# Two more features of each MLP's first group as half-size products, and the second mixer's block masks built from iotas in the second group

## The chip, the core and the metric

One NeuronCore of one Trainium2 chip runs the whole program. Its engines run side by side, each with a queue of its own: TensorE (PE: matrix products), VectorE (DVE), ScalarE (ACT), GpSimd (POOL), and SyncE (SP), which orders most DMAs. The metric is the device time of one execution in microseconds. The kernel before took 1311.64 us (median of three runs, 1311.3 to 1313.36).

## What is computed

Two residual layers of an encoder on 512 tokens of width 1024 in float32. Layer 0 mixes tokens with a bidirectional gated DeltaNet, layer 1 with gated linear attention (GLA). Behind each mixer comes a squared-ReLU MLP with 4096 features:

```python
def _sq_relu_mlp(h, w1, w2):
    a = jax.nn.relu(jnp.matmul(h, w1))
    return jnp.matmul(a * a, w2)

for i in range(DEPTH):                      # DEPTH = 2
    m = _mixer_gdn(...) if i % 2 == 0 else _mixer_gla(...)
    x = _layernorm(ALPHA * x + m, ln1_g[i], ln1_b[i])
    x = _layernorm(ALPHA * x + _sq_relu_mlp(x, mlp_w1[i], mlp_w2[i]), ln2_g[i], ln2_b[i])
```

GLA has a lower-triangular score matrix per chunk that the kernel builds by levels (blocks of 1, 2, 4 up to 64 positions); at each level a 0/1 mask of a 128x128 tile says which scores the level sets.

## The kernel before

**Split products.** Every float32 operand is split into a high half (a cast to fp32r, by ScalarE, L102) and a low half (what is left, by VectorE, L107). A product is then three matmuls: high by high, low by high, high by low (`mm3`, L128 to L130).

**The MLP** (function `mlp`) works in four groups of 1024 features; a group has 8 "features" (tiles of 128), f = 0 to 7 in the code. The up projection turns x (transposed, halves `xth` and `xtl`) into h; the down projection sums w2 times h into the residual `xt`.

- In groups 1 to 3 the up projection takes features in pairs (class `Pair`). Two features, the two halves of the 1024 inputs and the two halves of the 512 tokens make a 2x2 by 2x2 block product, and Strassen's scheme (in Winograd's form) does it in seven half-size products instead of eight. Each is 12 matmuls of 128x256. They are issued in the order 1, 2, 6, 5, 7, 3, 4; the text calls them P1 to P7. Their results go to two PSUM banks of tag `pj`, named `fx` and `fyz`. The products need sums of the blocks of x (`x_blocks`: four sums of high and low, L433, four combinations, L439 to L442, four splits into `xh` and `xl`), made once per MLP, and sums of the blocks of the weights, made per pair: `prepare` splits the first weight tile (P1, P2), forms four sums (L464) and splits one more half tile (P5, L470 and L471), then adds the last sum; `late(0, (6, 4))`, called by `finish`, splits the sum for P6 and P4; `late(1, (7, 3))` the one for P7 and P3.
- In group 0 the features 0 to 3 are computed as ordinary products in two halves of the tokens (`proj_halves`), and 4 to 7 one by one (`feature`): 8 tiles of the inputs by 3 matmuls of 128x512. Bank tag `pj`, results read by ScalarE (Relu L383, Square L384). While these run, VectorE and ScalarE make the x blocks and prepare the first pair.
- The down projection (`second`, `last`) uses the same scheme on the 2x2 blocks of h and w2, in seven products of four chunks of six matmuls of 128x512 (banks `pX`, `pY`, `pZ`). Blocks of w2 lie in tiles `w2r`, loaded by SyncE; their sums are formed by DMAs that GpSimd orders and that add in flight (L415). `split(1)` makes the halves (`w2h`, `w2l`) for the first product, `pair` those of h (`ah`, `al`).
- Chunks of group g's down projection are interleaved with products of group g+1 on TensorE.

**The order.** The code is recorded, and a scheduler then orders each engine's queue; `issue_after` and `high_priority` bend that. `in_order` pins the recorded order on one engine. Weight tiles come into a ring of three buffers (`wst`), halves go to a ring of three (`wh`, `wl`), and SyncE waits in its queue for a buffer to be free.

**The masks** (function `sel_masks`, called by `GlaConst` through `extra` of the first MLP): for each block size GpSimd fills a 128x128 tile with ones, cuts it twice by an affine select, subtracts the one before and casts to bytes. The call stands behind group 0; GpSimd starts it when the first MLP does.

Of the kernel before, what the change touches and what calls it, by code (L numbers as in the profile page):

```python
# [351 lines left out]
def mlp(c, w1, w2, g, b, out=None, extra=None, room=0):  # L352
# [14 lines left out]
    with c.banks(pj=2, X=2, Y=2, Z=2), tc.tile_pool(name="mlp", bufs=2) as pool:  # L367
# [333 lines left out]
        todo = [(gi, p) for gi in range(1, G) for p in range(GF // 2)]  # L701
# [23 lines left out]
        for f in range(4, GF):  # L725
            feature(0, f, h)
            if f >= 5:
                next(xb)
            if f == 4:
                load(0, 0, 0)  # L730
            if f == 5:
                load(0, 0, 1)
            if f == 6:
                load(0, 1, 1)
                with tc.issue_after(c.last_hi.ins), tc.issue_after(c.last_lo.ins):
                    split(1)
                a = pair(quarters(h)[0])
        begin(0)
        prepare(0)
        finish(0)  # L740
        if extra:
            extra(lambda: pool.tile([P, P], F32, name="tmp", tag="tmp", bufs=2))
        def stream(gi, nh):

            for p in range(GF // 2):
                i = (gi - 1) * (GF // 2) + p
                for n, _ in enumerate(ready[i].products(nh)):
                    if n == 0:
                        begin(i + 1)
                    elif n == 1:  # L750
                        ready[i].late(1, (7, 3))
                    elif n == 3:
                        prepare(i + 1)
                    elif n == 5:
                        finish(i + 1)
                    if p == 3 and n == 2 and gi + 1 == G:
                        load(gi, 1, 0, c.wst)
                    if p == 3 and n == 2:
                        split(1, None if gi + 1 < G else True)
                        stream.a = pair(quarters(nh)[0])  # L760
                    yield

        for gi in range(G - 1):
# [4 lines left out]
            with c.in_order(mybir.EngineType.PE):  # L768
                for i, _ in enumerate(second(gi, h, a)):
                    upto = n if i + 1 == m else min(i + 2, 7 * (i // 7) + 7) if i % 7 in (0, 2, 4, 6) else k  # L770
                    while k < upto:
                        next(more, None)
                        k += 1
                for _ in more:
                    pass
            h, a = nh, stream.a
        with c.in_order(mybir.EngineType.PE):
            norm, normed = last(G - 1, h, a)
# [6 lines left out]
def sel_masks(c, pool, tmp):  # L785

    nc = c.nc
    out = {}
    prev = None
    for w in (1, 2, 4, 8, 16, 32, 64, 128):  # L790
        f = tmp().rearrange("p (a b) -> p a b", b=w)
        nc.gpsimd.memset(f, 1.0)
        if w < P:
            nc.gpsimd.affine_select(out=f, in_=f, compare_op=ALU.is_ge, fill=0.0, base=0,
                                    pattern=[[-w, P // w], [0, w]], channel_multiplier=1)
            nc.gpsimd.affine_select(out=f, in_=f, compare_op=ALU.is_ge, fill=0.0, base=w - 1,
                                    pattern=[[w, P // w], [0, w]], channel_multiplier=-1)
        fl = f.rearrange("p a b -> p (a b)")
        if w != 2:
            m = pool.tile([P, P], mybir.dt.uint8, name=f"mu{w}", tag=f"mu{w}", bufs=1)  # L800
            if w == 1:
                nc.gpsimd.tensor_copy(m, fl)
            else:
                nc.gpsimd.tensor_tensor(prev, fl, prev, ALU.subtract)
                nc.gpsimd.tensor_copy(m, prev)
            out[w // 2] = m
        prev = fl
# [1106 lines left out]
```

## Time and profile before

| what | us |
|---|---|
| median of three runs | 1311.64 |
| the profiled execution | 1311.28 |
| its span on the core | 1309.6 |
| first MLP: features 4 to 7 of group 0 | 431.92 to 453.97 |
| second MLP: features 4 to 7 of group 0 | 1005.01 to 1027.09 |
| GpSimd building masks | 415.0 to 449.2 |
| first use of a mask by VectorE (L1042) | 760.3 |

The profile names a group of instructions by line, engine, operation and tiles (`out<-in`), with count, busy time and mean duration; `[x <-ENGINE tile line]` behind an instruction is the idle time of its engine just ahead of it and what ended that. A timeline gives the start and the duration of each instruction. A matmul's duration overlaps the next one's, so distances between starts tell its price. The windows give busy time of each engine between two moments.

### The profile page before, as it was taken

Reading aid. Unit: us, or ns where it says so; the run is one execution under the profiler, and the core shown is the slowest. Engines: PE = TensorE matmul, PEld = TensorE weight load, DVE = VectorE, ACT = ScalarE, POOL = GpSimd, SP = SyncE. Lnnn points to the kernel's source line nnn. Section 1 sums busy time; section 2 is a strip of 40 time slices with the busy share of each in tenths; the row PEclk is TensorE's granted clock in tenths of the full one; section 3 lists DMA queues with packets and bytes.
Section 4 is the critical chain, followed back from the end, with each engine's and each line's share of the span. In section 5 each row is a group of like instructions: output and inputs, shape, how many; then the busy total and the mean of one; then the engine's idle time right before and its main releaser. Section 6 shows DMA issues by size and latency. Waiting matters only on the chain.

```text
span 1309.6 us, 22228 instructions
## 1 busy us (share of the span) xinstructions
PE 1289.4 (98%) x8586; PEld 1106.3 (84%) x8586; DVE 1106.3 (84%) x1795; ACT 804.8 (61%) x1604; POOL 134.6 (10%) x190
## 2 busy tenths in 40 slices
PE   8999999999999999999999999999999999999996
PEld 6778888788878899999998888888888899999985
DVE  7888888988868998999989697877888789989987
ACT  5767676677543656666657754564456566666656
POOL 5000000000003710101102100000000001101021
PEclk9999999999999999999999999999999999999998
DMA  5333313233332664576647521211316376556565
GB/s 191 99 106 96 98 55 108 81 114 96 114 110 84 175 172 169 119 203 161 177 145 154 140 97 56 74 62 52 103 59 218 87 210 165 142 176 139 171 143 144
DMA packets 47805, 165.92 MB, mean 127 GB/s; under 512 B 5923, under 2 KB 6611, under 8 KB 47699
## 3 DMA queue, kind: packets, MB, share of 16 engines
q1 hardware_dynamic: 33603, 114.52, 25.8%
q0 software_dynamic: 13984, 49.95, 18.7%
q8 instruction: 67, 1.10, 0.3%
q14 instruction: 39, 0.32, 0.1%
q10 hardware_dynamic: 112, 0.03, 0.0%
HBM read 125.00 MB, written 2.65 MB: 97 GB/s over the span
## 4 chain that ended last, share of the span: by engine, by line
PE 91%; ACT 3%; DVE 3%; issue 1%; DMA 1%; SPq 0%; DVEq 0%; ACTq 0%
PE pjv L128 3%; PE pjv L129 3%; PE pjv L130 3%; PE pX L130 3%; PE pX L129 3%; PE fx L130 3%; PE fx L128 3%; PE fx L129 3%; PE pX L128 3%; PE m L1776 3%; PE fyz L128 3%; PE fyz L130 3%; PE fyz L129 3%; PE pY L129 2%; PE pY L130 2%; PE pY L128 2%
## 5 line engine op out<-in xcount | busy, mean ns | idle before, releaser
L102 ACT CAST wh<-wst 128x1024 fp32r<-128x1024 f32 x151 | 158.5, 1050 | 104.8 <-PE fyz L129 28.2
L107 DVE TENSOR_TENSOR wl<-wst,wh 128x1024 fp32r<-128x1024 f32 x149 | 183.2, 1232 | 40.3 <-ACT wh L102 40.2
L107 DVE TENSOR_TENSOR w2l<-w2r,w2h 128x1024 fp32r<-128x1024 f32 x92 | 111.5, 1222 | 21.6 <-ACT w2h L102 21.6
L102 ACT CAST w2h<-w2r 128x1024 fp32r<-128x1024 f32 x94 | 98.4, 1048 | 42.5 <-DMA w2r<-w2r 22.8
L415 POOL DMA_DIRECT2D w2r<-w2r x56 | 47.9, 887 | 492.9 <-DVE w2l L107 388.0
L464 DVE TENSOR_TENSOR wst<-wst 128x512 f32<-128x512 f32 x120 | 80.0, 687 | 0.8
L102 ACT CAST ah<-h 128x1024 fp32r<-128x1024 f32 x56 | 58.8, 1050 | 30.6 <-PE pY L129 12.0
L107 DVE TENSOR_TENSOR al<-h,ah 128x1024 fp32r<-128x1024 f32 x56 | 68.4, 1221 | 6.6 <-ACT ah L102 6.6
L130 PE MATMUL pX<-w2h,al 128*128 128x512 f32 x168 | 66.3, 394 | 0.0
L129 PE MATMUL pX<-w2l,ah 128*128 128x512 f32 x168 | 65.9, 392 | 0.0
L128 PE MATMUL pX<-w2h,ah 128*128 128x512 f32 x168 | 65.5, 390 | 0.0
L128 PE MATMUL pjv<-wh,xth 128*128 128x512 f32 x128 | 54.7, 428 | 0.0
L130 PE MATMUL fyz<-xh,wl 128*128 128x256 f32 x192 | 53.5, 278 | 0.0
L130 PE MATMUL fx<-xth,wl 128*128 128x256 f32 x192 | 53.4, 278 | 0.0
L128 PE MATMUL fyz<-xh,wh 128*128 128x256 f32 x192 | 53.4, 278 | 0.0
L128 PE MATMUL fx<-xth,wh 128*128 128x256 f32 x192 | 53.2, 277 | 0.0
L130 PE MATMUL fx<-xh,wl 128*128 128x256 f32 x192 | 53.2, 277 | 0.0
L129 PE MATMUL fx<-xtl,wh 128*128 128x256 f32 x192 | 53.2, 277 | 0.0
L129 PE MATMUL fyz<-xl,wh 128*128 128x256 f32 x192 | 53.1, 277 | 0.0
L129 PE MATMUL fx<-xl,wh 128*128 128x256 f32 x192 | 53.1, 277 | 0.0
L128 PE MATMUL fx<-xh,wh 128*128 128x256 f32 x192 | 53.1, 277 | 0.0
L129 PE MATMUL pj<-xtl,wh 128*128 128x256 f32 (+1 forms) x160 | 52.0, 326 | 0.2 <-DVE xtl L194 0.2
(542 smaller groups left out, 4312.7 us busy)
## 6 DMA issues: line engine op xcount, KB each, us to landing
wst<-in_w SPq DMA_DIRECT2D x68, 512.0 KB, 4.6
w2r<-in_w SPq DMA_DIRECT2D x60, 512.0 KB, 4.6
w2r<-w2r POOLq DMA_DIRECT2D x56, 512.0 KB, 5.7
wst<-in_a_in SPq DMA_DIRECT2D x31, 512.0 KB, 4.1
wst<-in_b_vr SPq DMA_DIRECT2D x16, 512.0 KB, 3.3
wst<-in_a_out SPq DMA_DIRECT2D x8, 512.0 KB, 4.6
wst<-in_b_in SPq DMA_DIRECT2D x8, 512.0 KB, 3.4
wst<-in_b_out SPq DMA_DIRECT2D x8, 512.0 KB, 3.2
```

Of the source, the lines that this page charges most:

```text
L102: h = nc.scalar.copy(hi, src)
L107: self.halves = h, nc.vector.tensor_tensor(lo, src, hi.bitcast(F32), ALU.subtract)
L128: mm(ps, ah, bh, start=start, stop=False, **kw)
L129: mm(ps, ah, bl, start=False, stop=False, **kw)
L130: self.last_mm = mm(ps, al, bh, start=False, stop=stop, **kw)
L415: nc.gpsimd.dma_start(blocks[a + (q,)], blocks[b + (q,)], accum_op=ALU.add)
L464: plus = lambda a, b: V.tensor_tensor(a, a, b, ALU.add)
L1776: T.matmul(ps[:, d, :], *ops(d), start=True, stop=True)
```

## The change

Features 6 and 7 of group 0 become a pair: it stands first in the list of pairs (`todo`), and its seven products run right behind feature 5, with no chunks between. The steps that prepare the following pair (`begin`, `late`, `prepare`, `finish`) are called from the pair's products as in the later groups (`step`). Two calls of `x_blocks` move ahead by a feature, and the loads and the split of the first w2 blocks move behind `finish(0)`. One `in_order` now spans TensorE's whole stretch from these products to the end of the down projection. The masks are built differently: GpSimd writes the block number of each column with an iota, VectorE shifts the row numbers into block numbers of the rows, and one VectorE comparison per level gives the mask (equal for blocks of 1, unequal for the larger ones). This is called in the second group (gi == 0, behind its chunks, issued after the first split there). Only the first MLP builds masks; both MLPs get the new pair.

```diff
-        todo = [(gi, p) for gi in range(1, G) for p in range(GF // 2)]
+        todo = [(0, GF // 2 - 1)] + [(gi, p) for gi in range(1, G) for p in range(GF // 2)]
...
+        def step(i, n):
+            if n == 0:
+                begin(i + 1)
+            elif n == 1:
+                ready[i].late(1, (7, 3))
+            elif n == 3:
+                prepare(i + 1)
+            elif n == 5:
+                finish(i + 1)
+
-        for f in range(4, GF):
+        for f in (4, 5):
             feature(0, f, h)
-            if f >= 5:
-                next(xb)
-            if f == 4:
-                load(0, 0, 0)
-            if f == 5:
-                load(0, 0, 1)
-            if f == 6:
-                load(0, 1, 1)
-                with tc.issue_after(c.last_hi.ins), tc.issue_after(c.last_lo.ins):
-                    split(1)
-                a = pair(quarters(h)[0])
+            next(xb)
+            load(0, 0, f - 4)
         begin(0)
+        next(xb)
         prepare(0)
         finish(0)
-        if extra:
-            extra(lambda: pool.tile([P, P], F32, name="tmp", tag="tmp", bufs=2))
+        load(0, 1, 1)
+        with tc.issue_after(c.last_hi.ins), tc.issue_after(c.last_lo.ins):
+            split(1)
+        a = pair(quarters(h)[0])
+        whole = contextlib.ExitStack()
+        whole.enter_context(c.in_order(mybir.EngineType.PE))
+        for n, _ in enumerate(ready[0].products(h)):
+            step(0, n)
...
+            if extra and gi == 0:
+                with tc.issue_after(c.halves[1].ins):
+                    extra(lambda: pool.tile([P, P], F32, name="tmp", tag="tmp", bufs=2))
...
+    G.iota(pi, pattern=[[0, n]], base=0, channel_multiplier=1)
+    for k in range(1, n):
+        V.tensor_scalar(pi[:, k:k + 1], pi[:, k:k + 1], k, None, ALU.arith_shift_right)
+    V.tensor_copy(pf, pi)
...
+    for k in range(n):
+        w = 1 << k
+        f = tmp()
+        G.iota(f.rearrange("p (a b) -> p a b", b=w), pattern=[[1, P // w], [0, w]], base=0, channel_multiplier=0,
+               allow_small_or_imprecise_dtypes=True)
+        m = out[w if k else 0] = pool.tile([P, P], mybir.dt.uint8, name=f"mu{w}", tag=f"mu{w}", bufs=1)
+        V.tensor_scalar(m, f, pf[:, k:k + 1], None, ALU.not_equal if k else ALU.is_equal)
```

**VectorE, first MLP, from the last combination of x blocks.** In the kernel before (`xl` low halves of the x blocks, `wl` of up-projection weights, `al` of h, `w2l` of w2; L464 the sums of the pair's weights):

```order
L442 SCALAR_TENSOR_TENSOR w2r<-w2r 128x1024
L107 TENSOR_TENSOR al<-h,ah 128x1024
L107 TENSOR_TENSOR wl<-wst,wh 128x1024
L107 TENSOR_TENSOR xl_6041<-w2r,xh_6040 128x1024
L107 TENSOR_TENSOR xl_6045<-w2r,xh_6044 128x1024
L107 TENSOR_TENSOR xl_6049<-w2r,xh_6048 128x1024
L107 TENSOR_TENSOR wl<-wst,wh 128x1024
L464 TENSOR_TENSOR wst<-wst 128x512 x4
L107 TENSOR_TENSOR w2l<-w2r,w2h 128x1024
L471 TENSOR_TENSOR wl<-wst,wh 128x512
L464 TENSOR_TENSOR wst<-wst 128x512
L107 TENSOR_TENSOR wl<-wst,wh 128x1024
```

In the changed kernel, from the same instruction to the low half for P6 (the last row):

```order
L442 SCALAR_TENSOR_TENSOR w2r<-w2r 128x1024
L107 TENSOR_TENSOR wl<-wst,wh 128x1024
L107 TENSOR_TENSOR xl_5961<-w2r,xh_5960 128x1024
L107 TENSOR_TENSOR xl_5969<-w2r,xh_5968 128x1024
L464 TENSOR_TENSOR wst<-wst 128x512
L107 TENSOR_TENSOR w2l<-w2r,w2h 128x1024
L464 TENSOR_TENSOR wst<-wst 128x512 x2
L471 TENSOR_TENSOR wl<-wst,wh 128x512
L464 TENSOR_TENSOR wst<-wst 128x512 x2
L107 TENSOR_TENSOR w2l<-w2r,w2h 128x1024
L107 TENSOR_TENSOR al<-h,ah 128x1024
L107 TENSOR_TENSOR wl<-wst,wh 128x1024
```

The low halves of features 6 and 7 are gone from this queue, and the splits for the down projection (`w2l`, `al`) now stand between the pair's sums and P6's low half. From the first L433 to that row, the changed queue holds 18 instructions of 1024 elements and 6 of 512. In the second MLP P6's low half has 20 of 1024 and 6 of 512 ahead of it from the first L433 on, two of them splits that stood elsewhere.

**ScalarE, first MLP, from the Relu of the last feature before the pair's half tile.** In the kernel before (`wh` L470 the half tile of the pair, Relu L383 and Square L384 of features 6 and 7 around it):

```order
L383 ACTIVATE h<-pj 128x512
L384 ACTIVATE h<-h 128x512
L102 CAST w2h<-w2r 128x1024
L470 CAST wh<-wst 128x512
L383 ACTIVATE h<-pj 128x512
L384 ACTIVATE h<-h 128x512
L102 CAST wh<-wst 128x1024
L383 ACTIVATE h<-pj 128x512
```

In the changed kernel (the first Relu is feature 4's, the second feature 5's; the `w2h` is the first half of the block of the down projection's second product, the `wh` behind the second Relu the high half for P6, L499 and L506 copy P1 and P6):

```order
L383 ACTIVATE h<-pj 128x512
L384 ACTIVATE h<-h 128x512
L470 CAST wh<-wst 128x512
L102 CAST w2h<-w2r 128x1024
L383 ACTIVATE h<-pj 128x512
L102 CAST wh<-wst 128x1024
L384 ACTIVATE h<-h 128x512
L499 COPY h<-fx 128x256
L102 CAST wh<-wst 128x1024
L522 ACTIVATE h<-h 128x256
L506 COPY h<-fx 128x256
```

The cast of `w2h` now stands ahead of the Relu that frees P2's bank and of P6's high half; its block is ordered by SyncE when the third x block has been split. In the second MLP the same cast stands ahead of L470 and of both Relus, and the high half for P6 ahead of feature 5's Relu.

**VectorE, start of the second group of the first MLP.** In the kernel before (`wl` of the next pair, L577 and L579 combinations of the blocks of h, L503 adds P2):

```order
L107 TENSOR_TENSOR w2l<-w2r,w2h 128x1024
L107 TENSOR_TENSOR wl<-wst,wh 128x1024
L577 TENSOR_TENSOR h<-h 128x4x256
L107 TENSOR_TENSOR al<-h,ah 128x1024
L503 TENSOR_TENSOR h<-h,fyz 128x256
L579 SCALAR_TENSOR_TENSOR h<-h 128x4x256
L107 TENSOR_TENSOR wl<-wst,wh 128x1024
L107 TENSOR_TENSOR w2l<-w2r,w2h 128x1024
```

In the changed kernel (`pi` the row numbers, `pf` the same as float, `tmp` the iotas, `mu` the masks; three more comparisons follow):

```order
L797 TENSOR_SCALAR pi<-pi 128x1 x6
L577 TENSOR_TENSOR h<-h 128x4x256
L798 CAST pf<-pi 128x7
L107 TENSOR_TENSOR al<-h,ah 128x1024
L503 TENSOR_TENSOR h<-h,fyz 128x256
L806 TENSOR_SCALAR mu_6931<-tmp,pf 128x128
L806 TENSOR_SCALAR mu_6935<-tmp,pf 128x128
L107 TENSOR_TENSOR wl<-wst,wh 128x1024
L806 TENSOR_SCALAR mu_6939<-tmp,pf 128x128
L806 TENSOR_SCALAR mu_6943<-tmp,pf 128x128
L107 TENSOR_TENSOR w2l<-w2r,w2h 128x1024
```

The mask work stands between the splits, and L579 has moved behind all seven comparisons. The first two iotas are made when the MLP starts; the other five wait for a comparison to free a tile. On TensorE the order differs in one place per MLP: 84 matmuls of 128x256 (`fx`, `fyz`) where 48 of 128x512 (`pj`) stood, between feature 5 and the first `pX`.

More of the change, by code (lines that the diff above doesn't have):

```diff
@@ L767, in mlp @@
             m = 24 if gi + 2 == G else 28
[L768 to L775, printed above, removed]
-            h, a = nh, stream.a
-        with c.in_order(mybir.EngineType.PE):
-            norm, normed = last(G - 1, h, a)
+            for i, _ in enumerate(second(gi, h, a)):
+                upto = n if i + 1 == m else min(i + 2, 7 * (i // 7) + 7) if i % 7 in (0, 2, 4, 6) else k
+                while k < upto:
+                    next(more, None)
+                    k += 1
+            for _ in more:
+                pass
+            h, a = nh, stream.a
+            if extra and gi == 0:
+                with tc.issue_after(c.halves[1].ins):
+                    extra(lambda: pool.tile([P, P], F32, name="tmp", tag="tmp", bufs=2))
+        norm, normed = last(G - 1, h, a)
+        whole.close()
         with contextlib.nullcontext() if out is not None else tc.issue_after(normed[1].ins):
```

35 lines of the change are left out of this document (6 added, 29 removed).

## The prediction

> **What bounds the kernel now.** I read the page's first part, then the table of windows over the stretch that changes, then TensorE's timeline there.
>
> ```profile
> PE 1289.4 (98%) x8586; PEld 1106.3 (84%) x8586; DVE 1106.3 (84%) x1795; ACT 804.8 (61%) x1604; POOL 134.6 (10%) x190
> PE 91%; ACT 3%; DVE 3%; issue 1%; DMA 1%; SPq 0%; DVEq 0%; ACTq 0%
> ...
> core 0: us, PE busy (x) PEld busy (x) DVE busy (x) ACT busy (x) POOL busy (x), PEclk, DMA share, GB/s
> 432.00:454.00 22.00, 22.00 (x98) 18.03 (x97) 20.90 (x20) 13.11 (x18) 17.79 (x21) 1.00 0.64 195
> 532.00:572.00 40.00, 40.00 (x263) 36.29 (x262) 36.95 (x46) 25.51 (x37) 4.25 (x5) 1.00 0.66 160
> 572.00:612.00 40.00, 40.00 (x266) 36.42 (x265) 36.13 (x45) 26.17 (x38) 2.56 (x3) 1.00 0.62 171
> 1005.00:1028.00 23.00, 23.00 (x102) 18.82 (x101) 13.13 (x14) 11.84 (x16) 1.70 (x2) 1.00 0.76 230
> ```
>
> TensorE has 91% of the chain that ended last, and in the MLPs it is busy in every microsecond of these windows at full clock. So a matmul removed there is worth its own time, and any new wait is worth its own length. The windows also show the difference on which this case turns. In the first MLP (432 to 454 us) VectorE is busy 20.90 of 22 us; in the second (1005 to 1028) 13.13 of 23.
>
> **What goes: matmul time.** TensorE's timeline gives the starts: features 6 and 7 of the first group, the chunk of the down projection behind them, then P1, P2 of the next pair and the chunk behind (columns: start, duration, engine, line, operation).
>
> ```profile
> 442.94 0.40 PE L128 MATMUL pj<-xth,wh 128*128 128x512 f32 x1
> 453.97 0.39 PE L128 MATMUL pX<-w2h,ah 128*128 128x512 f32 x1
> ...
> 455.36 0.28 PE L128 MATMUL fx<-xth,wh 128*128 128x256 f32 x1
> 456.72 0.28 PE L128 MATMUL fyz<-xth,wh 128*128 128x256 f32 x1
> 458.09 0.39 PE L128 MATMUL pX<-w2h,ah 128*128 128x512 f32 x1
> ...
> 1016.08 0.39 PE L128 MATMUL pj<-xth,wh 128*128 128x512 f32 x1
> 1027.09 0.39 PE L128 MATMUL pX<-w2h,ah 128*128 128x512 f32 x1
> ```
>
> The two features take 453.97 - 442.94 = 11.03 us (second MLP 11.01), which is 48 matmuls of 512 columns at 0.230 us. A product of 12 matmuls of 256 columns takes (458.09 - 455.36) / 2 = 1.365 us, 0.114 us each, so seven take 9.55 us. The gain is 1.48 us per MLP, **2.95 us** in both, if TensorE never waits.
>
> The Trainium skill (TensorE: Matmul & The Clock Gate, section Back-to-back issue gap) speaks against such halving. It gives about 81 ns per matmul at 128 columns and about 131 at 512 in a sustained stream; interpolated, an estimate of mine, 256 columns would take 98, three quarters of a full one, and the seven products would lose 84 x 0.098 - 48 x 0.131 = 1.9 us per MLP. The trace here does not agree: its matmuls are in proportion to their columns (0.114 against 0.230), both widths are in its rows, and so this gets no chance of its own.
>
> **What comes: VectorE's chain to P6 in the first MLP.** Features 6 and 7 were also the 11 us in which VectorE finished the sums of x and the weights of the first pair. P6, third product, needs its low half of the weights (the last row of the new VectorE order shown ahead) 2 x 1.365 us and two matmuls after P1. P1 starts where feature 6 did, at 442.94, so this low half is due at 442.94 + 2.73 + 0.23 = 445.9. From the first sum of x (L433) the new order has 18 instructions of 1024 elements and 6 of 512 ahead of it. Their pace:
>
> ```profile
> 421.94 3.92 DVE L433 TENSOR_TENSOR w2r<-xth,xtl 128x1024 f32<-128x1024 f32 x3
> ...
> 1000.27 1.22 DVE L107 TENSOR_TENSOR xl<-w2r,xh 128x1024 fp32r<-128x1024 f32 x1
> 1001.41 1.22 DVE L107 TENSOR_TENSOR wl<-wst,wh 128x1024 fp32r<-128x1024 f32 x1
> ...
> 468.55 1.28 DVE L464 TENSOR_TENSOR wst<-wst 128x512 f32<-128x512 f32 x2
> ...
> 455.08 1.23 DVE L107 TENSOR_TENSOR wl<-wst,wh 128x1024 fp32r<-128x1024 f32 x1 [1.17 <-ACT wh L102]
> ...
> L107 DVE TENSOR_TENSOR wl<-wst,wh 128x1024 fp32r<-128x1024 f32 x5 | 6.8, 1357 | 0.0
> L433 DVE TENSOR_TENSOR w2r<-xth,xtl 128x1024 f32<-128x1024 f32 x4 | 5.3, 1357 | 0.0
> ...
> L107 DVE TENSOR_TENSOR wl<-wst,wh 128x1024 fp32r<-128x1024 f32 x3 | 3.6, 1215 | 0.0
> L433 DVE TENSOR_TENSOR w2r<-xth,xtl 128x1024 f32<-128x1024 f32 x4 | 4.7, 1217 | 0.0
> ...
> L804 POOL TENSOR_TENSOR tmp<-tmp x6: 552/1292/1374, 423.6 to 448.0; 128x128 f32<-128x128 f32 x6
> ```
>
> The last groups are the same lines in the first MLP (421.9 to 447.2 us, 1357 ns) and in the second (988.9 to 1010.6, 1215 ns). GpSimd builds the masks beside the first, 423.6 to 448.0, and nothing beside the second, though there more bytes are moving (230 GB/s against 195). I take it that the masks slow VectorE, and that with them gone it goes at 1.14 us from start to start, as at 1000.27 and 1001.41, and 0.60 for 512 elements (1.28 - 0.68 for the second of two).
> The Trainium skill (SBUF — State Buffer, section SBUF: two separate sides) says that VectorE and GpSimd share one pair of SBUF ports as an exclusive lock, which a VectorE instruction with two SBUF inputs meets when GpSimd reads SBUF too. By that rule the pace is 1.14 here, since only iotas are left and those run later; without it, 1.28, and the chain is 2.5 us longer. The trace agrees so far as the two groups show.
>
> Sum: 18 x 1.14 + 6 x 0.60 = 24.1 us, plus about 0.4 us where an instruction needs the one just ahead of it or ScalarE's cast, from 421.94: the low half starts at 446.4, ends at 447.65, and its load into TensorE starts the matmul at about 447.9. P6 is late by 447.9 - 445.9 = **2.0 us**. Nothing covers it, for TensorE's queue is in fixed order and the next products stand behind P6. They find their halves ready: P7's low half is the VectorE instruction but one after P6's, and P7 comes 1.365 us after P6's end. P6 of the next pair is due 5 steps of about 1.37 us behind the chunk at 454.5, at 461.5; its second block is ordered when P6's low half ends (447.65), lands 5.4 us later (below) at 453.1, five sums, a half tile's split and one addition to h take it to 457.2, two instructions of 1024 to 459.5, its low half to 461.0. First MLP: +2.0 - 1.48 = **+0.5 us**.
>
> **The load in ScalarE's way.** In the new ScalarE order a cast of a down-projection block (w2h) that has just been ordered stands ahead of the Relu of feature 5 and of the high half for P6; ScalarE stops there until it lands.
>
> ```profile
> w2r<-in_w SPq DMA_DIRECT2D x4, 512.0 KB, 4.9
> ...
> w2r<-in_w SPq DMA_DIRECT2D x1, 512.0 KB, 8.7
> ...
> 450.27 1.05 ACT L102 CAST w2h<-w2r 128x1024 fp32r<-128x1024 f32 x1 [5.16 <-DMA w2r<-in_w]
> 451.74 0.59 ACT L383 ACTIVATE h<-pj 128x512 f32<-128x512 f32 x1
> 452.37 0.63 ACT L384 ACTIVATE h<-h 128x512 f32<-128x512 f32 x1
> ```
>
> Such loads landed after 4.9 us (437 to 447) and 8.7 (one at 1003.8). In the first MLP it is ordered when the third x block is split, near 437.9; cast, Relu and high half take 2.6 us, so a landing of up to 5.9 us costs nothing, and each microsecond more costs one. I take 5.4, between the rows and nearer to the first.
>
> **The second MLP.** Here VectorE had time.
>
> ```profile
> 988.92 1.22 DVE L433 TENSOR_TENSOR w2r<-xth,xtl 128x1024 f32<-128x1024 f32 x1
> ...
> 1009.36 1.21 DVE L107 TENSOR_TENSOR xl<-w2r,xh 128x1024 fp32r<-128x1024 f32 x1
> ...
> 1017.42 1.22 DVE L107 TENSOR_TENSOR w2l<-w2r,w2h 128x1024 fp32r<-128x1024 f32 x1 [4.66 <-ACT w2h L102]
> ```
>
> Its x blocks were done at 1010.6 and it idled 4.66 us before 1017.42. P1 starts at 1016.08, and P6's low half is due at 1019.0. From 988.92 the new order has 20 instructions of 1024 and 6 of 512 ahead of it, 26.4 us and some 1.5 of waits, so it could start at 1016.8; its high half waits for feature 5's last matmuls (buffer), 1016.0 + 1.05, so it starts near 1017.1 and ends by 1018.3, 0.7 us in time. The Relu of feature 5, behind that cast, frees P2's bank at 1017.54, 0.15 us late. The load again: ordered near 1005.2, it must land within 6.8 us; four others are ordered in the 5.7 us before it, so it is nearer its limit than the first, and I take it as met. Second MLP: -1.48 + 0.15 = **-1.33 us**.
>
> **The masks.** GpSimd's mask instructions of the first group go, at no gain but the pace above, since TensorE never waited for them. VectorE gets 6 shifts, a conversion and 7 comparisons inside the second group.
>
> ```profile
> L206 DVE TENSOR_SCALAR rst<-rst x28: 132/154/170, 116.8 to 1303.4; 128x1 f32<-128x1 f32 x16, 128x4 f32<-128x4 f32 x12
> L1783 DVE SCALAR_TENSOR_TENSOR r<-m,neg,vt x48: 340/343/352, 89.2 to 380.8; 128x128 f32<-128x128 f32 x48
> L792 POOL MEMSET tmp<- x8: 205/206/218, 415.0 to 447.7; 128x128 f32 x8
> ```
>
> By these rows 7 x 0.15 + 7 x 0.34 = 3.4 us. No row shows an iota: between a memset's 0.21 us and 1.29 for L804 above; five of them alternate with comparisons through two buffers, so VectorE waits for them 0 to 3.5 us. I take 0, nearest the memset, an operation that reads nothing either. The windows from 532 have 3.05 and 3.87 us of VectorE idle time, and what is pushed back is needed some 4 us later or more, so 3.4 us cost nothing on TensorE; with no cover they would cost 3.4, with slow iotas about 2.5 beyond the cover.
>
> **Sum.** +0.5 - 1.33 + 0 = -0.8 us. The profiled execution took 1311.28 us (span 1309.6 and 1.7 around it), so 1310.5; the median of the runs, 1311.64, lies 0.36 above it, which would give 1310.8. I say **1310.6**. A change below 0.2% (2.6 us) is about what a measurement of this kernel cannot tell from none.
>
> **Rivals.**
> - *P6 finds its halves in time in both MLPs*, because ScalarE or VectorE runs ahead of my chain: -2.95 + 0.15, so **1308.6**. For it: VectorE's pace without masks is my inference, and 2.0 us is 8% of the chain. Against it: 24 us of instructions from 421.94 cannot end at 445.9 unless a pace better than 1.14 appears, and no row has one.
> - *The block's load lands late*, the mechanism that ends slower: with 8.7 us in both MLPs ScalarE stops 2.8 us beyond the limit in the first and 1.9 in the second: -0.8 + 4.7 gives **1315.3**; it decides from 5.9 and 6.8 us on, and passes +0.2% when both are over 8.2 us. For it: the row of 8.7 us. Against: beside that load ran the two accumulating DMAs below, which in the new order follow the block's split, near 1009.
>
> ```profile
> 998.78 0.87 POOL L415 DMA_DIRECT2D w2r<-w2r  x1 [110.97 <-DVE w2l L107]
> 999.86 0.87 POOL L415 DMA_DIRECT2D w2r<-w2r  x1 [0.21 <-issue]
> ```
>
> - *VectorE's slow pace is not the masks'*: chain +2.5 us, **1313.1**.
> - *The masks overflow in the second group*: +2.5, **1313.1**.
>
> **Chances.** Forecast 0.60 (its own range 1309.1 to 1312.2), all in time 0.20, late loads 0.10, slow pace 0.06, masks 0.04. Faster by over 0.2% (below 1309.0) is the second case, with a little of it missing the bound: 0.20. Slower by over 0.2% (above 1314.3) is most of the late loads: 0.08. Range: 1308.4 takes in the second case, 1313.7 the last two and the milder late loads; the loads at 8.7 us stay outside.
>
> **What would show it.** Right: in the first MLP VectorE's lines near 422 to 447 at 1.22 us, not 1.36; TensorE waiting near 446 about 2 us for wl (L107) at the P6 product, and nowhere in the second MLP beyond 0.2 us; no TensorE wait from 532 to 612. Wrong: no wait at P6 (then my chain is too long), a wait for wh or for the Relu behind a DMA (then the load decides), or waits in the second group (then the masks do).

## The result and the profile after

The changed kernel took **1319.64 us** (median of 6 runs, 1318.93 to 1320.56) beside 1311.47 us for the kernel before on the same chip (6 runs): a ratio of 1.0061, interval 1.0048 to 1.0074, slower by 8.2 us. The forecast was 1310.6 us, its range ended at 1313.7.

The page of the changed kernel, busy time and chain of waits:

```profile
PE 1295.4 (98%) x8658; PEld 1111.1 (84%) x8658; DVE 1116.6 (85%) x1829; ACT 809.1 (61%) x1616; POOL 109.1 (8%) x163
PE 87%; DVE 6%; ACT 4%; issue 1%; DMA 1%; SPq 0%; DVEq 0%; ACTq 0%
```

Its windows where the prediction read them:

```profile
432.00:454.00 22.00, 21.23 (x131) 18.73 (x130) 20.65 (x25) 15.17 (x24) 2.69 (x3) 1.00 0.77 212
532.00:572.00 40.00, 40.00 (x258) 36.15 (x258) 36.09 (x56) 23.23 (x33) 5.76 (x10) 1.00 0.64 153
572.00:612.00 40.00, 39.14 (x250) 35.15 (x249) 36.21 (x47) 26.17 (x37) 2.60 (x3) 1.00 0.55 164
1005.00:1028.00 23.00, 23.00 (x151) 20.70 (x150) 19.91 (x22) 18.16 (x27) 3.48 (x4) 1.00 0.91 243
```

The waits that the prediction looked for are small: in the first MLP (440 to 690 us) TensorE waited for these, and in the second (1000 to 1290) for nothing (columns: in all, times, longest, us):

```profile
PE fyz L128 <- ACT h L523: 0.9, 1, 0.9
PE fx L130 <- DVE wl L107: 0.5, 1, 0.5
PE fyz L128 <- ACT h L383: 0.2, 1, 0.2
```

They are 1.6 us of 8.2. The window from 532 shows the rest in another way: TensorE is busy for all of its 40 us at full clock, as before, but 258 matmuls start in it where 263 did. The matmuls themselves are further apart. TensorE's timeline of the first MLP shows it: a chunk of 12 matmuls (`pY`), two products of 12 (`fx`, `fyz`) and the next chunk; before first, the changed kernel behind it.

```profile
477.44 0.39 PE L128 MATMUL pY<-w2h,ah 128*128 128x512 f32 x1
480.18 0.28 PE L128 MATMUL fx<-xh,wh 128*128 128x256 f32 x1
481.54 0.28 PE L128 MATMUL fyz<-xh,wh 128*128 128x256 f32 x1
482.91 0.39 PE L128 MATMUL pY<-w2h,ah 128*128 128x512 f32 x1
```

```profile
477.50 0.40 PE L128 MATMUL pY<-w2h,ah 128*128 128x512 f32 x1
480.30 0.28 PE L128 MATMUL fx<-xh,wh 128*128 128x256 f32 x1
481.73 0.28 PE L128 MATMUL fyz<-xh,wh 128*128 128x256 f32 x1
483.15 0.39 PE L128 MATMUL pY<-w2h,ah 128*128 128x512 f32 x1
```

The chunk took 2.74 us and takes 2.80, a product 1.36 and 1.43. Nothing waits in these rows. To see where this adds up, the time is cut at starts that both traces have (us):

| stretch | before | after |
|---|---|---|
| A: first MLP, output of the first mixer to the first `pX` | 67.5 | 68.1 |
| B: first `pX` to the first `pX` of the last group | 234.8 | 240.3 |
| C: to the first gate matmul of the mixer (`gps`) | 38.8 | 39.0 |
| D: the mixer, to its first output matmul (`ob` from `v`) | 232.9 | 234.1 |
| E: second MLP, as A, from that output | 66.7 | 65.9 |
| F: second MLP, as B | 234.8 | 236.1 |
| G: second MLP, last group, to the last matmul | 35.8 | 36.1 |

Stretches A and E, on which the prediction spent its working, came out at +0.6 and -0.8 us (forecast +0.5 and -1.33). B, D and F together are 8.2 us longer (5.6, 1.3 and 1.4); the rest nearly cancels: A, C and G add 1.1, E takes off 0.8, and the profiled execution is 0.9 us shorter ahead of A and 0.7 longer behind the last matmul, whose causes stay open. The 588 chunk matmuls on w2 blocks of the first MLP, 516 of them in B, stand 233.3 ns apart where they stood 230.0 (+1.7 us in B), the 1008 of the products in B 117.7 for 114.9 (+2.9 us, waits left out), and 0.9 us are waits. In F the chunks went from 229.9 to 233.4 ns (+1.8 us), and the products from 114.9 to 114.5 (-0.4 us).

What else did the change move? The compiled program gives each tile a byte address in SBUF, the same in all partitions. The pool hands addresses out in the order in which tiles are first asked for. The changed code asks for the x blocks ahead of the first split of w2, so the two swapped places, and the two new index tiles (`pi`, `pf`) move everything of the first MLP and of the mixer by 64 bytes:

```
                      before: first, second MLP    after: first, second MLP
ah, first buffer      120352    119328             120416    119328
w2h, first buffer     169504    168480             202432    201344
xh for P5             194176    193152             169664    168576
```

### The profile page after: what moved, and what is told of

The parts are those of the page before. It is cut to its first block, busy times and chain, and to the rows that moved or that the text cites. A ratio compares the mean times of both kernels' runs of the same rounds, so it can differ in the third digit from the quotient of the medians.

```text
span 1317.8 us, 22382 instructions
## 1 busy us (share of the span) xinstructions
PE 1295.4 (98%) x8658; PEld 1111.1 (84%) x8658; DVE 1116.6 (85%) x1829; ACT 809.1 (61%) x1616; POOL 109.1 (8%) x163
## 4 chain that ended last, share of the span: by engine, by line
PE 87%; DVE 6%; ACT 4%; issue 1%; DMA 1%; SPq 0%; DVEq 0%; ACTq 0%
PE fx L130 4%; PE fx L128 4%; PE fx L129 4%; PE pjv L128 3%; PE pjv L129 3%; PE pjv L130 3%; PE pX L129 3%; PE pX L128 3%; PE pX L130 3%; PE m L1775 3%; PE fyz L128 3%; PE fyz L130 3%; PE fyz L129 3%; PE pY L129 2%; PE pY L128 2%; PE pY L130 2%
## 5 line engine op out<-in xcount | busy, mean ns | idle before, releaser
L107 DVE TENSOR_TENSOR wl<-wst,wh 128x1024 fp32r<-128x1024 f32 x151 | 184.7, 1226 | 38.8 <-ACT wh L102 38.3
L107 DVE TENSOR_TENSOR w2l<-w2r,w2h 128x1024 fp32r<-128x1024 f32 x92 | 111.2, 1219 | 17.5 <-ACT w2h L102 17.5
L415 POOL DMA_DIRECT2D w2r<-w2r x56 | 48.5, 898 | 519.8 <-DVE w2l L107 233.3
L464 DVE TENSOR_TENSOR wst<-wst 128x512 f32<-128x512 f32 x130 | 86.2, 684 | 0.9 <-DMA wst<-in_w 0.4
L107 DVE TENSOR_TENSOR al<-h,ah 128x1024 fp32r<-128x1024 f32 x56 | 68.2, 1219 | 7.2 <-ACT ah L102 7.2
L130 PE MATMUL fx<-xh,wl 128*128 128x256 f32 x208 | 58.2, 280 | 0.5 <-DVE wl L107 0.5
L128 PE MATMUL fyz<-xh,wh 128*128 128x256 f32 x208 | 58.5, 281 | 0.0
L128 PE MATMUL fx<-xh,wh 128*128 128x256 f32 x208 | 58.3, 280 | 0.0
L129 PE MATMUL fx<-xl,wh 128*128 128x256 f32 x208 | 58.2, 280 | 0.0
L130 PE MATMUL fyz<-xh,wl 128*128 128x256 f32 x208 | 58.2, 280 | 0.0
L129 PE MATMUL fyz<-xl,wh 128*128 128x256 f32 x208 | 58.1, 279 | 0.0
L128 PE MATMUL fx<-xth,wh 128*128 128x256 f32 x208 | 57.9, 278 | 0.0
L129 PE MATMUL fx<-xtl,wh 128*128 128x256 f32 x208 | 57.8, 278 | 0.0
L130 PE MATMUL pjv<-wh,xtl 128*128 128x512 f32 x128 | 50.3, 393 | 0.0
```

Source lines behind the costliest of these rows:

```text
L107: self.halves = h, nc.vector.tensor_tensor(lo, src, hi.bitcast(F32), ALU.subtract)
L128: mm(ps, ah, bh, start=start, stop=False, **kw)
L129: mm(ps, ah, bl, start=False, stop=False, **kw)
L130: self.last_mm = mm(ps, al, bh, start=False, stop=stop, **kw)
L415: nc.gpsimd.dma_start(blocks[a + (q,)], blocks[b + (q,)], accum_op=ALU.add)
L464: plus = lambda a, b: V.tensor_tensor(a, a, b, ALU.add)
```

## First four runs: is it the addresses, and is it their remainder by 128?

*Theory A*: the pace follows where the operands stand. *Rival B*: the changed work and its order slow TensorE. Padding of 64 bytes in the mixer's constants and of 32 behind the x blocks changes addresses alone, but for a memset of each pad:

```diff
+        nc.vector.memset(pool.tile([P, 16], F32, name="pad", bufs=1), 0.0)   # GlaConst: phases_back, pad_only, before_64
...
+            gap(32)                                # x_blocks, behind its splits: phases_back, w2gap_only
```

> The changed kernel with 64 bytes of padding in the mixer's constants and 32 bytes behind the x blocks, so that h, ah, al, the x blocks, the w2 ring and the mixer's tiles stand at the same offsets modulo 128 bytes as in the kernel before; no other work changes. Theory A (the matmuls' own pace hangs on where their operands stand in SBUF): 1309.5 to 1311.5 us, the 512-column chunk matmuls 0.230 us apart in both MLPs, where the changed kernel has 0.2333. Rival B (the changed work, its queues and its order slow TensorE): 1319 to 1320 us and 0.2333, as the changed kernel.

> The changed kernel with the 64 bytes of padding in the mixer's constants alone: ah and the x blocks are back at their offsets modulo 128 in the first MLP (32 and 0), the w2 ring is at 0 in both MLPs where the kernel before had 32. Theory A: 1315 to 1317 us; the products of the first MLP are 1.36 us again for 12 matmuls, the chunk matmuls stay at 0.2333 us in both MLPs. Rival B: 1319 to 1320 us.

> The kernel before with 64 bytes of padding in the mixer's constants, which move every tile of the first MLP and of the mixer by 64 bytes (modulo 128: ah and the w2 ring from 32 to 96, the x blocks from 0 to 64); no work is changed but one memset of 16 columns. Theory A: 1313 to 1316 us, the products over x blocks at 1.42 us for 12 matmuls in the first MLP and nothing changed in the second MLP. Rival B: 1311.5 us, no change.

> The changed kernel with 32 bytes behind the x blocks alone: the w2 ring is at 32 modulo 128 in the second MLP as before, at 96 in the first (64 in the changed kernel), the rest stands as in the changed kernel. Theory A: 1314.5 to 1317.5 us; the chunk matmuls of the second MLP are 0.230 us apart, the products of the first MLP stay at 1.42 us. Rival B: 1319 to 1320 us.

| run | us | ratio to before | A | B | D | F |
|---|---|---|---|---|---|---|
| phases_back | 1321.26 | 1.0083 (1.0069 to 1.0096) | 67.9 | 238.6 | 233.8 | 237.5 |
| pad_only | 1319.04 | 1.0061 (1.0048 to 1.0075) | 67.9 | 239.5 | 233.7 | 236.1 |
| before_64 | 1313.83 | 1.0020 (1.0011 to 1.0029) | 67.4 | 237.3 | 232.8 | 234.8 |
| w2gap_only | 1321.52 | 1.0081 (1.0067 to 1.0094) | 68.0 | 240.2 | 233.4 | 237.5 |

The expectations for phases_back, pad_only and w2gap_only missed. The remainder by 128 isn't the rule: with all remainders as before, phases_back gained 1.7 us in B and lost 1.4 in F. But before_64 speaks clearly for addresses: 64 bytes of padding, no work moved, and B takes 2.5 us more; F, where nothing moved, is untouched. (In phases_back, w2gap_only and, further down, pair_alone about 2 us are lost in the first 40 us of the program, where TensorE's granted clock was 0.96 for 1.00; the stretches leave that out, and its cause stays open.)

## Next four: the whole placement, and the parts alone

layout_back does the changed kernel's work with the tiles at their old addresses; before_layout does the old work with the changed kernel's addresses. (In both, a few mask tiles stand elsewhere, and which buffer of a ring a tile comes to goes with the work.) Two runs do one part of the change each, at the old addresses.

```diff
 # layout_back: first w2 buffers asked for ahead of the x blocks; pi and pf at the end of the MLP's pool
+            early.extend((None, *[pool.tile([P, 2, 512], F32R, name=n, tag=n, bufs=3) for n in ("w2h", "w2l")], 0) for q in range(2))
...
-    pi = pool.tile([P, n], mybir.dt.int32, name="pi", bufs=1)
+    pi, pf = tmp(n, mybir.dt.int32, "pi", 1), tmp(n, F32, "pf", 1)
 # before_layout: the x blocks' tiles asked for when x_blocks starts, and the pad of 64 bytes
+            homes_ = {i: [pool.tile([P, KT // 2, HT], F32R, name=n + str(i), tag=n + str(i), bufs=1) for n in ("xh", "xl")] for i in (5, 6, 7, 3)}
```

> The changed kernel with every SBUF tile at the address it had in the kernel before: the first two tile pairs of the w2 ring are taken from the pool ahead of the x blocks, and the two index tiles of the masks stand at the end of the MLP's pool; the work and the PE order are the changed kernel's. Theory A2 (the matmuls' pace hangs on the whole placement of their operands against each other, not on the offset modulo 128 alone): 1309 to 1311 us, the chunk matmuls 0.230 us apart again. Rival B (the changed order of work slows them): 1319 to 1321 us and 0.233.

> The kernel before with the placement of the changed kernel: 64 bytes of padding in the mixer's constants, and the x blocks' tiles taken from the pool ahead of the w2 ring; no work moves. Theory A2: 1317 to 1319.5 us (1313.8 us with the 64 bytes alone, and about 11 ns more for each chunk step of three matmuls, 196 steps in each of two MLPs, 4.4 us), chunk matmuls 0.2333 us apart in both MLPs. Rival B: 1311 to 1314 us and 0.230.

> The two features as seven products, the masks by GpSimd at their old place, every tile at its address of the kernel before. Theory A2: 1310 to 1313 us: the 1.48 us of matmul time saved in each MLP, against a wait in the first MLP that is longer than in the changed kernel, since the masks now run beside the VectorE chain (1.36 us an instruction there for 1.22). Rival B: 1318 us or more.

> The masks by iota and VectorE in the second group, the features as before, every tile at its address of the kernel before. Theory A2: 1310.5 to 1312.5 us, no change that can be told. Rival B': the masks in the second group are what slows the matmuls: 1314 us or more.

| run | us | ratio to before | A | B | D | E | F |
|---|---|---|---|---|---|---|---|
| layout_back | 1315.99 | 1.0036 (1.0023 to 1.0048) | 67.9 | 238.3 | 233.9 | 65.9 | 234.6 |
| before_layout | 1318.76 | 1.0058 (1.0045 to 1.0070) | 67.4 | 239.3 | 232.8 | 66.7 | 237.5 |
| pair_alone | 1318.40 | 1.0049 (1.0036 to 1.0063) | 70.9 | 236.1 | 233.6 | 65.9 | 234.7 |
| masks_alone | 1313.31 | 1.0017 (1.0008 to 1.0026) | 67.6 | 236.4 | 232.9 | 66.7 | 234.8 |

before_layout came out as expected; layout_back, pair_alone and masks_alone missed their ranges. (pair_alone has its rival's time, but not by the rival's pace: its matmuls stand 230.0 and 114.8 ns apart, and 2 us are lost at the start of the program and 3.5 in A.) before_layout is the plainest run of the study: the old work at the new addresses is 7.3 us slower. The chain of waits on its page still has TensorE at 91%:

```profile
PE 91%; ACT 3%; DVE 3%; DMA 1%; issue 1%; SPq 0%; DVEq 0%; ACTq 0%
```

And TensorE's timeline at the place shown above has the changed kernel's distances (2.79, 1.44, 1.43 us):

```profile
478.06 0.40 PE L128 MATMUL pY<-w2h,ah 128*128 128x512 f32 x1
480.85 0.28 PE L128 MATMUL fx<-xh,wh 128*128 128x256 f32 x1
482.29 0.28 PE L128 MATMUL fyz<-xh,wh 128*128 128x256 f32 x1
483.72 0.39 PE L128 MATMUL pY<-w2h,ah 128*128 128x512 f32 x1
```

layout_back has the old pace again (chunks 229.9 and 230.4 ns, products 115.0 and 114.0), but missed its 1309 to 1311: it is still 4.5 us slower than before. Matmul by matmul its stretch B differs from that of its own second MLP, which runs the same sequence, by waits: 1.0 us in the first third, 2.2 from 564 to 576 us; 0.5 us are spread evenly. In the changed kernel less of this is seen: its distances beyond the pace sum to 1.3 us in B, those of layout_back to 3.7 (0.2 in the kernel before). The two differ in addresses alone, so slower matmuls seem to have given the other engines time. So the two losses don't add up; placement alone costs 7.3 us on the old work and 3.7 on the new (8.2 less 4.5).

Those from 564 on belong to the masks: in B masks_alone has TensorE's distances of the kernel before to 0.01 us up to there, and then loses 1.7 us. The timeline shows GpSimd's queue (DMAs that sum blocks of w2) and ScalarE's casts of those sums, before and in masks_alone:

```profile
551.17 1.72 POOL L415 DMA_DIRECT2D w2r<-w2r  x2 [14.39 <-DVE w2l L107]
...
560.23 1.05 ACT L102 CAST w2h<-w2r 128x1024 fp32r<-128x1024 f32 x1 [1.99 <-DMA w2r<-w2r]
```

```profile
552.45 1.76 POOL L415 DMA_DIRECT2D w2r<-w2r  x2 [12.09 <-ACT h L523]
...
561.44 1.05 ACT L102 CAST w2h<-w2r 128x1024 fp32r<-128x1024 f32 x1 [2.88 <-DMA w2r<-w2r]
```

TensorE's waits in masks_alone, 440 to 615 us (the kernel before has none):

```profile
PE fyz L128 <- ACT h L523: 1.1, 1, 1.1
```

The summing DMA is ordered 1.3 us later, ScalarE stands before the cast until the sum has landed, 1.2 us later, and the Relu (L523) for which `fyz` waits stands behind it in ScalarE's queue. What made the DMA late is not the time of the mask instructions. From start to start they take some 1.8 us of VectorE's queue, and by the last sums of the weights (L464) the lag is made up: 548.12 for 548.00 us. But VectorE's queue has another order there, before and in masks_alone:

```profile
544.39 1.22 DVE L107 TENSOR_TENSOR al<-h,ah 128x1024 fp32r<-128x1024 f32 x1
...
548.00 1.29 DVE L464 TENSOR_TENSOR wst<-wst 128x512 f32<-128x512 f32 x2
549.20 2.35 DVE L107 TENSOR_TENSOR w2l<-w2r,w2h 128x1024 fp32r<-128x1024 f32 x2
```

```profile
548.12 1.28 DVE L464 TENSOR_TENSOR wst<-wst 128x512 f32<-128x512 f32 x2
549.33 1.22 DVE L107 TENSOR_TENSOR al<-h,ah 128x1024 fp32r<-128x1024 f32 x1
550.46 2.35 DVE L107 TENSOR_TENSOR w2l<-w2r,w2h 128x1024 fp32r<-128x1024 f32 x2
```

L579 stands behind the masks, and the split `al`, which stood well ahead of the sums, stands right ahead of the two `w2l` that release the summing DMA. (The second GpSimd row names the Relu L523 as what ended the wait; but before, this Relu ends at 551.94, after the DMA's start, and in both kernels the DMA starts 0.8 us behind the end of the first `w2l`.) The changed kernel and layout_back have the same order there.

pair_alone shows the price of GpSimd's masks beside the pair: A is 3.0 us longer than in layout_back, and VectorE's group of L433 (here L434) is at the slow pace:

```profile
L434 DVE TENSOR_TENSOR w2r<-xth,xtl 128x1024 f32<-128x1024 f32 x4 | 5.3, 1358 | 0.0
```

In the changed kernel, without those masks, it is 1219 ns (below). The Trainium skill (SBUF — State Buffer, section SBUF: two separate sides) has VectorE and GpSimd share one pair of ports; these two rows agree with it.

## Four more: two mechanisms, one place at a time

```diff
 # second_only: the pair in the second MLP alone, old masks, old addresses
+        todo = ([(0, GF // 2 - 1)] if out is not None else []) + [(gi, p) for gi in range(1, G) for p in range(GF // 2)]
 # masks_spread (old features, old addresses): one mask in every fourth step of the second group
+                    if extra and gi == 0 and i % 4 == 1:
+                        with tc.issue_after(c.halves[1].ins):
 # w2_shift (the kernel before): less padding ahead of the x blocks, which so stay in the first MLP; the shift ahead of the first split of w2
-            gap(96)
+            gap(64 if room else 96)
...
+                gap(32 if room else 1024)
 # idle_56 (the kernel before): idle matmuls at the start of the program
-            for i in range(20):
+            for i in range(56):
```

> The seven products for features 7 and 8 in the second MLP alone; the first MLP and the masks are those of the kernel before, and every tile stands at its address of the kernel before. Theory: the second MLP gains what it gained with the old placement (1.0 us from the mixer's end to the last group), and neither the first MLP's waits nor the 1.0 us at the mixer's end come back, since TensorE's instruction stream is unchanged up to there: 1310.0 to 1310.9 us beside 1311.4. Rival: what is saved is lost again behind it (a wait or a load that falls badly): 1311.4 us.

> The masks by iota and VectorE as in the run with the masks alone, but one mask in every fourth step of the second group and behind a cast of its own each, not all in one place. Theory C (a lump of 3.4 us on VectorE makes the cast that releases the summing transfers late): the 1.3 us wait of TensorE falls below 0.6 us, 1311.4 to 1312.6 us. Rival D (VectorE has no room for 3.4 us anywhere in this group): 1313 us or more.

> The kernel before with the w2 ring moved against ah, and no work changed but three memsets: by 32 bytes in the first MLP, by 1024 bytes in the second. In the kernel before the two stand a multiple of 4096 bytes apart. Theory A3 (the pace hangs on how far the moving operand stands from the stationary one, in steps below 1024 bytes): the chunk matmuls go from 0.230 to 0.232 or 0.234 us in the first MLP, 1.2 to 2.4 us, and stay at 0.230 in the second: 1312.6 to 1314 us. Rival: both MLPs change (it is the whole distance that counts, 1314 to 1316 us), or neither (1311.4 us; it was the order of the rings).

> The kernel before with 56 for 20 of the idle matmuls at the start, so that TensorE has executed 36 matmuls more by the time of the mixer, as the changed kernel has there. Theory F (the 1 us at the mixer's end comes from the place of TensorE's instruction fetches, which meet the landing of a weight block): the stretch from the first gate matmul to the first output matmul is 233.6 to 234.1 us, where the kernel before takes 232.9. Rival: 232.9, the wait comes from something that the first MLP leaves behind. The start is some 5 to 8 us longer, so that the whole time says nothing.

| run | us | ratio to before | B | D | E | F |
|---|---|---|---|---|---|---|
| second_only | 1311.95 | 1.0004 (0.9995 to 1.0013) | 234.7 | 233.0 | 65.8 | 236.2 |
| masks_spread | 1311.65 | 1.0002 (0.9993 to 1.0011) | 234.7 | 232.9 | 66.7 | 234.8 |
| w2_shift | 1313.97 | 1.0016 (1.0007 to 1.0025) | 237.5 | 232.8 | 66.7 | 234.8 |
| idle_56 | 1314.05 (one run) | | 234.7 | 233.9 | 66.7 | 235.7 |

*w2_shift*: moved by 32 bytes against `ah`, the w2 ring costs the first MLP 2.7 us; moved by 1024 (and the x blocks with it), it costs the second nothing. At the place of the rows above the chunk takes 2.79 us in the first MLP (first two rows), and a chunk of the second takes the old 2.77 (last two):

```profile
478.43 0.39 PE L128 MATMUL pY<-w2h,ah 128*128 128x512 f32 x1
481.22 0.28 PE L128 MATMUL fx<-xh,wh 128*128 128x256 f32 x1
...
1054.17 0.39 PE L128 MATMUL pY<-w2h,ah 128*128 128x512 f32 x1
1056.94 0.28 PE L128 MATMUL fx<-xh,wh 128*128 128x256 f32 x1
```

The products of the first MLP slowed too (114.9 to 116.6 ns) though neither of their operands had moved a byte against the other; what a product finds seems to hang on the chunk ahead of it as well. What the hardware does there is not shown.

*masks_spread*: the same masks on the same engine cost nothing when they don't come in one lump; stretch B is that of the kernel before, and so is VectorE's order at the place above. So it was the lump, through the order that came with it; that order without the lump was not run.

*idle_56* settles stretch D. In the changed kernel ScalarE waits there for a block of weights (`wst`), and `kdt` behind it holds TensorE up. The DMA view of that moment (GB/s in 40 slices of a window of 5 to 7 us, and the queue of instruction fetches), before, in layout_back and in idle_56:

```profile
GB/s 0 0 0 0 0 0 0 0 0 0 98 229 393 262 197 328 393 328 393 393 328 393 328 99 33 0 0 0 0 0 0 0 0 0 0 0 66 0 0 0
q14 instruction: 1, 0.01, 0.7%
```

```profile
GB/s 0 0 0 0 0 0 0 0 104 156 130 286 312 494 416 312 390 390 208 26 26 0 0 26 0 26 26 26 26 26 26 0 0 0 0 0 0 0 0 0
q8 instruction: 1, 0.02, 1.2%
```

```profile
GB/s 0 0 0 0 0 0 0 0 0 0 0 0 187 164 70 211 538 421 328 351 304 257 70 23 23 0 23 23 23 23 23 23 0 0 0 0 0 0 0 0
q8 instruction: 1, 0.02, 1.1%
```

What TensorE waited for behind it in idle_56, a wait that the kernel before does not have:

```profile
PE stp L1078 <- ACT kdt L1068: 0.7, 1, 0.7
```

The load of 512 KB ends in a tail of single packets where a fetch of 16 KB from the queue q8 falls into it. In the trace such a packet takes 1.2 us on one of the 16 DMA engines; in layout_back 15 parts of the load have landed at 211.9 us after the first gate matmul, the sixteenth at 213.8 (in the changed kernel the sixteenth at 214.0; before: all by 212.0, the fetch at 217.5). The 36 matmuls more of the first MLP put the fetch there, and 36 idle ones at the start do the same to the old kernel: D is 233.9. (Its F is 0.9 us longer too, by late starts of two `fyz` products, at 1147.9 and 1225.8 us, whose cause stays open. Its start is 0.7 us longer, not the 5 to 8 expected.)

*second_only* has B and D of the kernel before and gains 0.9 us in E, as expected, and yet no time: F is 1.4 us longer, so its range was missed and the rival's 1311.4 is nearer.

## The last three

Which slot of the ring of `wh` and `wl` a product's weights come to has changed as well, since a pair asks for other tiles than two features do. In the second MLP the 11 distances between a product's 12 starts sum to 1.246 us in most cases and to 1.296 in others, and which it is goes mostly with the x block and the slot. Two runs move the slots by sending weights of features to the ring of `ah`; the third is the whole change, with old addresses and spread masks.

```diff
 # slot_one (slot_two: f >= 4), on second_only
-                feature(0, f, h)
+                feature(0, f, h, c.wcols(w1, f * P, pool=ring("ah")) if f == 5 else None)
```

> The seven products in the second MLP alone, as before, but feature 6 takes its weights into the ring of ah (at its own place there), so that every later product of that MLP finds its weights one slot further on in the ring of wh and wl. Theory G (in that kernel the second MLP's stream took 236.2 us for 234.8 because its products met other slots: 1.29 us for 12 matmuls over x6 and the first rows of the right half in slot 1, 1.25 in slot 2): the stream is 234.6 to 235.0 us again and the time 1310.2 to 1310.9 us. Rival: 236.2 us and no gain, 1311.4 to 1312 us, the loss comes from the work.

> The same with features 5 and 6 both in the ring of ah, two slots further on. Theory G: another value between 234.5 and 236.3 us for the second MLP's stream, with the same matmuls and the same waits. Rival: 236.2 us in this one too.

> The whole change with every tile at its address of the kernel before and one mask in every fourth step of the second group: what is left of the change without its placement and its lump of masks. From the parts: 1311.4 us, 0.4 us lost ahead of the stream, 1.0 us in the first MLP's stream (waits after the pair), 1.0 us at the mixer's end, 1.0 us gained in the second MLP: 1312.3 to 1313.8 us. Rival (the placement hid other losses): 1315 us or more.

| run | us | ratio to before | A | B | D | E | F |
|---|---|---|---|---|---|---|---|
| slot_one | 1311.68 | 1.0001 (0.9993 to 1.0010) | 67.6 | 234.7 | 233.0 | 65.8 | 235.3 |
| slot_two | 1310.98 | 1.0000 (0.9991 to 1.0009) | 67.6 | 234.7 | 233.0 | 65.7 | 235.8 |
| all_repaired | 1314.63 | 1.0025 (1.0016 to 1.0035) | 67.9 | 237.4 | 233.5 | 65.9 | 234.5 |

In the second MLP the products stand 115.6 ns apart in second_only, 114.9 in slot_one and slot_two, and 114.0 in layout_back, all at the same addresses but for the slot, and F followed. Distances beyond the pace take back a part: they sum to 0.8 us in second_only and slot_one and to 1.2 in slot_two, 0.2 before. slot_one missed both of its ranges; slot_two's F lies in its own. Neither time can be told from that of the kernel before. all_repaired missed its range by 0.8 us: B is 237.4 for an expected 236. Its distances beyond the pace sum to 2.7 us there, those of pair_alone, without VectorE's masks, to 1.7. So beside the pair's waits even the spread masks seem not to be free; whether by their time or by the order was not separated. No version found here beats the kernel before by more than can be measured.

## Why the prediction was wrong, by its own steps

- **"So a matmul removed there is worth its own time"** is the step that failed, or rather what it left out: that the matmuls that stay keep their pace, 0.230 and 0.114 us. They went to 0.233 and, in the first MLP, 0.118, because the order in which the new code asks for tiles moves them in SBUF. before_layout shows 7.3 us for that with no other change, against a whole range of 5.3. No rival had it. On the new work it is 3.7 us: layout_back, with the old pace, still takes 1316.0, above the range, so the forecast would have missed by the terms below too.
- *First MLP, +0.5*: came out at +0.6 in stretch A, and for the most part by the mechanism forecast. VectorE went at 1.22 us an instruction instead of 1.36 (row below), and the low half for P6 starts 24.2 us after the first L433 (421.06 to 445.23), where the forecast had 24.1 and 0.4. Its matmul comes 1.6 us behind its due moment (P1's 441.97 and 2.96 us; 446.51), where the forecast had 2.0. Only 0.5 us of this shows as a wait for `wl` (L107), because P2's wait for a Relu and smaller gaps had made P6 0.9 us late already. In all the seven products take 2.1 us more than 9.55, 1.7 in waits and gaps and 0.4 by the pace of the 84 matmuls (1.30 us for 11 distances of P1, from 441.97 to 443.27); that the pace fills up the forecast's 2.0 is luck.
- *Second MLP, -1.33*: -0.8 in E, right in sign and mechanism; no waits, as said. The seven products took 10.1 us there, not 9.55 and 0.15, by small gaps at the starts of P2 and P3.
- *The load in ScalarE's way*: the rival did not occur. ScalarE waited 2.6 us at that cast (row below), and 0.2 us of it reached TensorE through the Relu (L383).
- *The masks, 0*: wrong by 1.7 us. The idle time of VectorE that I counted as cover (3.05 and 3.87 us of 40) was there, and it covered the masks' own time, some 1.8 us where the forecast had 3.4. But the lump also changed the order behind it, so that a split (`w2l`) that a summing DMA waits for came 1.3 us later, and behind that DMA stand a cast, a Relu and TensorE. "What is pushed back is needed some 4 us later or more" did not hold for that split. The rival's 2.5 us stood for slow iotas; VectorE waited for none, so that its price lies near is luck.
- *Not considered*: waits of the pair further back in B (1.0 us in layout_back) and the instruction fetch in D (1.0 us).

P6 in the changed kernel: VectorE's first L433, the low half, and the matmul that waits for it:

```profile
421.06 3.49 DVE L433 TENSOR_TENSOR w2r<-xth,xtl 128x1024 f32<-128x1024 f32 x3
...
445.23 1.22 DVE L107 TENSOR_TENSOR wl<-wst,wh 128x1024 fp32r<-128x1024 f32 x1
...
446.51 0.39 PE L130 MATMUL fx<-xh,wl 128*128 128x256 f32 x1 [0.52 <-DVE wl L107]
```

VectorE's groups of the first MLP in the changed kernel (421 to 447 us):

```profile
L107 DVE TENSOR_TENSOR wl<-wst,wh 128x1024 fp32r<-128x1024 f32 x5 | 6.1, 1218 | 0.0
L433 DVE TENSOR_TENSOR w2r<-xth,xtl 128x1024 f32<-128x1024 f32 x4 | 4.7, 1219 | 0.0
```

ScalarE's timeline there:

```profile
442.16 1.05 ACT L102 CAST w2h<-w2r 128x1024 fp32r<-128x1024 f32 x1 [2.61 <-DMA w2r<-in_w]
```

What stays open: why these distances in SBUF cost what they cost, and what makes the first products of a pair slow in some slots; the runs show only that they do.

## What to carry to other kernels

Where one engine is busy all the time, an edit that moves no work can still change the price of each instruction: compare the addresses of the tiles before and after as one compares the order, and test a placement by itself (padding, or the order of first use) before blaming the work. Idle time can cover the length of added instructions and yet not the new order of the queue behind them: look up which transfer waits for that engine next, and what now stands ahead of it. And when a trace shows a wait far from the edit, look at what the longer instruction stream fetches at that moment.

## What was not expected of the hardware

- 32 bytes between the moving and the stationary operands' tiles cost 2.7 us in one MLP, some 2 ns on each of 516 matmuls of 512 columns and 1 to 2 on each of 1008 of 256; 1024 bytes cost nothing. The same product takes 1.246 or 1.296 us, mostly by its x block and the buffer that its weights came to.
- One instruction fetch of 16 KB delayed the sixteenth part of a load by 1.8 us and TensorE by 1.0.
- Where the matmuls were slower, waits were shorter: distances beyond the pace take 1.3 us in stretch B of the changed kernel, and 3.7 with the old addresses.
